# A two-layer decoder trunk: the mixer's token norm folded into the split operands

## The chip, the cores and the metric

The kernel runs on one NeuronCore of a Trainium2 chip. The metric is device microseconds of one execution, as the median of several runs. TensorE (PE in the profile) multiplies, with its own rows for weight loads (PEld); VectorE is DVE, ScalarE is ACT, GpSimd is POOL. SyncE (SP) issues nearly all DMA transfers, in the order in which they stand in its queue.

## The reference

Two layers work on x of 1024 tokens by 1024 features, in float32. What the change touches is the first part of a layer, the mixer:

```python
h = rmsnorm(x, norm_mix[l])                       # x * rsqrt(mean(x*x) + EPS) * g
proj = jnp.einsum('btd,de->bte', h, w_in[l])      # 1024 -> 4352
q, k, v, u, ug, ga, gb = jnp.split(proj, SPLITS, axis=-1)
q = partial_rope(rmsnorm(q, q_norm[l]), cos, sin) # per head of 64
k = partial_rope(rmsnorm(k, k_norm[l]), cos, sin)
a_out = sliding_window_attention(q, k, v, sinks[l])
c_out = conformer_conv(u, ug, ...)                # a = u * sigmoid(ug); depthwise conv of width 31; layernorm; silu; projection
merged = sigmoid(ga) * a_out + sigmoid(gb) * c_out
x = x + merged @ w_out[l]
```

A gated feed-forward with its own norm (`norm_ffn`, `w_gate_up`, `w_down`) follows and adds to x. Features lie on partitions in the kernel, tokens along the free axis, so x is eight tiles of 128 x 1024.

## The kernel before

**Precision.** Each float32 operand is split into a high part in fp32r (a rounded copy, made by ACT) and the remainder (a subtraction). `mm3` (L236) forms a product from three matmuls per step and half of the tokens: high by high, high by low, low by high. For weights, `fetch` (L120) loads a raw tile of 512 KB, ACT copies it to `wh` (L133) and POOL subtracts to `wl` (L134); there are two raw tiles, three of `wh` and two of `wl` (L1159).

**Stages of a layer.** The input projection has 34 column tiles, in the order of `INPROJ` (L1138); a tile is eight contraction steps of six matmuls, into a PSUM tile of 128 x 1024 out of a ring of two. The mixer's attention and its convolution run beside these tiles. Then come the two projections to x (`wcv`, `wout`), the feed-forward's up products and its down products, the last in seven block products p1 to p7 of which p3 is the last (L1124).

**The norm.** x is split after the product with the gain g, and without the token factor r = rsqrt(mean + eps): r is one number per token, and so can be put on a column of the result. In layer 0, `split_g` (L281) makes the two parts from each loaded tile of x, POOL squares the tile, DVE adds the squares to `acc` (L288). In layer 1 the same is done with half tiles as the down products release them (`done`, L1051): the tile goes to DRAM, ACT and DVE make the two parts, ACT squares, DVE adds. `norm_a` (L370) then takes token means by TensorE (`tokmean`, one column per 128 tokens), a power of -0.5 by POOL, a diagonal by DVE (`diag`, L308), and a product with a matrix of ones that spreads r over the partitions into the tile `R` of 128 x 1024. Values, conv values, conv gates and both sets of gates are multiplied by R as DVE takes them out of PSUM (L451, L473, L478, L724); ACT then makes the sigmoids in SBUF (L479, L725), and POOL multiplies conv value and gate (L482). Queries and keys aren't multiplied: their own norm per head cancels r, if its eps is scaled, which `e64` does (L373, L394).

**The first tiles.** Keys and values are computed together, step by step (L739 to L752). In layer 0 the steps follow the order of the loaded tiles; in layer 1 the first four steps are 4 to 7 in both halves, then the rest by halves, since p3 completes the tiles 0 to 3 of the second token half last.

**What sets the order.** TensorE's instructions are always in program order, as is DVE's from the first keys to the end of the attention (L754). The other engines' order comes from a planner that simulates the program with its own costs. Within the attention stage the program order is made from a clock written by hand: `tick()` (L227) advances it by one at each contraction step, and runs the events that are due; `after`, `at` and `when_free` set such events. The 32 attention units (four for each pair of heads) start 16 ticks after the first query tile, one every 6 ticks (L779). A unit computes scores into PSUM, DVE takes the maxima, ACT the exponentials, TensorE transposes, POOL masks the two parts by four selects (L684, L687), TensorE multiplies by the values. A query tile brings its own work: eviction and squares by ACT, four DMA moves for the rotation, two products and a power on POOL, sums and splits on DVE. The convolution is 31 taps for each of four tiles on DVE (L492, L496), one every 1.42 ticks, from 2 ticks after the first conv gate, when the tile `a` is handed over (6 ticks after the gate).

## Time and profile before

| | |
|---|---|
| median of three runs | 2698.68 us (2694.47 to 2700.15) |
| the profiled execution's own time | 2704.77 us |
| span in its profile | 2703.0 us |
| mean granted TensorE clock | 0.975 |
| busy: TensorE, DVE, ACT, POOL | 2588.6, 1843.6, 1190.6, 1601.5 us |
| first query tile leaves PSUM (layer 0, layer 1) | 96.11, 1437.67 us |

The rows of the profile give start, duration, engine, line, operation, output and inputs with their sizes; in square brackets stands the idle time before the instruction and what ended it. Rows of groups give count, busy time and mean duration, then that idle time. Matmuls are pipelined: two of them may overlap, so their pace is read from a run of many.

### The profile page before, as it was taken

How to read it: one execution, taken by the hardware profiler on the slowest of the kernel's cores; microseconds unless marked ns; L12 is line 12 of the kernel's file. 1: busy time of each engine (PE TensorE's matmuls, PEld its weight loads, DVE VectorE, ACT ScalarE, POOL GpSimd, SP SyncE). 2: the span in 40 equal slices, each digit the busy share in tenths (PEclk: the TensorE clock that was granted, in tenths of full speed). 3: DMA queues.
4: the chain of work that ended last, by engine and by line, in shares of the span. 5: the costliest groups of instructions: out<-in, count | busy, mean ns of one | idle time of the engine just before them, and what ended most of it. 6: DMA issues, size and time to landing. Idle time of an engine off the chain costs nothing.

```text
span 2703.0 us, 33316 instructions
## 1 busy us (share of the span) xinstructions
PE 2588.6 (96%) x11736; PEld 2118.2 (78%) x11736; DVE 1843.6 (68%) x2037; ACT 1190.6 (44%) x2299; POOL 1601.5 (59%) x1028
## 2 busy tenths in 40 slices
PE   7999999999999999999999999989999999999999
PEld 5777777788787888878777777778887788888887
DVE  6689998552567777845637899895616678778344
ACT  2266666742432323344523566668425222223443
POOL 7368776525256767765534777775252677767544
PEclk8999999999999999999999999989999999999999
DMA  3222222475244454476721222234752444455666
GB/s 129 57 66 58 82 80 67 158 271 208 90 164 147 168 179 156 160 269 218 238 67 52 65 88 65 74 93 156 252 203 94 179 168 146 162 179 193 223 223 210
DMA packets 137478, 395.83 MB, mean 146 GB/s; under 512 B 16160, under 2 KB 16416, under 8 KB 137312
## 3 DMA queue, kind: packets, MB, share of 16 engines
q1 hardware_dynamic: 137168, 393.63, 43.3%
q8 instruction: 92, 1.51, 0.2%
q14 instruction: 74, 0.61, 0.1%
q10 hardware_dynamic: 144, 0.09, 0.0%
HBM read 259.17 MB, written 115.34 MB: 139 GB/s over the span
## 4 chain that ended last, share of the span: by engine, by line
PE 64%; DVE 21%; DMA 4%; POOL 4%; issue 3%; ACT 2%; SPq 1%; DVEq 0%; ACTq 0%; POOLq 0%
PE b L850 40%; PE ps L242 20%; DVE y L496 9%; DVE mx L652 1%; DVE sc L648 1%; DVE q L610 1%; DVE acc L295 1%; DVE A L714 1%; DMA qs<-q 1%; PE po L702 1%; POOL q L385 1%; DVE pl L679 1%; DVE g L724 1%; DMA x<-xs 1%; POOL wl L134 1%
## 5 line engine op out<-in xcount | busy, mean ns | idle before, releaser
L151 POOL TENSOR_TENSOR plo<-fraw,phi 128x512 fp32r<-128x512 f32 x290 | 421.4, 1461 | 232.5 <-ACT phi L149 217.4
L134 POOL TENSOR_TENSOR wl<-raw,wh 128x1024 fp32r<-128x1024 f32 (+1 forms) x100 | 241.0, 2411 | 292.2 <-PE ps L242 250.3
L151 POOL TENSOR_TENSOR plo<-fs,phi 128x512 fp32r<-128x512 f32 x160 | 264.7, 1665 | 252.0 <-ACT phi L149 240.4
L496 DVE SCALAR_TENSOR_TENSOR y<-a,vec,y 128x1024 f32<-128x1024 f32 x240 | 402.6, 1678 | 3.6
L149 ACT CAST phi<-fraw 128x512 fp32r<-128x512 f32 x444 | 257.6, 618 | 246.7 <-POOL plo L151 133.6
L242 PE MATMUL ps<-hx,wh 128*128 128x512 f32 x1056 | 350.6, 414 | 7.2 <-ACT hx L283 7.2
L242 PE MATMUL ps<-lx,wh 128*128 128x512 f32 x1056 | 341.0, 405 | 0.8 <-DVE lx L284 0.8
L242 PE MATMUL ps<-hx,wl 128*128 128x512 f32 x1056 | 337.4, 401 | 4.5 <-POOL wl L134 4.5
L149 ACT CAST phi<-fs 128x512 fp32r<-128x512 f32 x160 | 95.4, 620 | 533.9 <-DVE fs L164 520.1
L151 DVE TENSOR_TENSOR plo<-fraw,phi 128x512 fp32r<-128x512 f32 x154 | 129.8, 848 | 191.5 <-ACT phi L149 189.3
L242 PEld LDWEIGHTS ps<-hx,wl 128*128 128x128 f32 x1056 | 206.7, 196 | 50.8 <-POOL wl L134 4.9
L850 PE MATMUL b<-plo,phi 128*128 128x512 f32 x616 | 241.1, 391 | 4.5 <-DVE plo L151 4.2
L242 PEld LDWEIGHTS ps<-lx,wh 128*128 128x128 f32 x1056 | 207.6, 197 | 48.3 <-DVE lx L284 1.5
L850 PE MATMUL b<-phi,plo 128*128 128x512 f32 x616 | 240.4, 390 | 0.0
L850 PE MATMUL b<-phi 128*128 128x512 f32 x616 | 240.4, 390 | 0.0
L242 PEld LDWEIGHTS ps<-hx,wh 128*128 128x128 f32 x1056 | 196.1, 198 | 43.1 <-ACT hx L283 7.2
L133 ACT CAST wh<-raw 128x1024 fp32r<-128x1024 f32 (+1 forms) x100 | 98.1, 981 | 175.7 <-PE ps L242 137.1
L656 ACT ACTIVATE sc<-sc,nm,fq 128x129 f32<-128x129 f32 x256 | 123.8, 486 | 70.4 <-DVE nm L654 69.9
L918 POOL TENSOR_TENSOR g<-g,u 128x512 f32<-128x512 f32 (+1 forms) x84 | 129.3, 1557 | 31.6 <-DVE u L971 25.2
L914 DVE TENSOR_TENSOR g<-g 128x512 f32<-128x512 f32 x88 | 103.9, 1181 | 62.8 <-POOL g L918 42.5
L850 PEld LDWEIGHTS b<-plo,phi 128*128 128x128 f32 x616 | 116.1, 188 | 31.8 <-DVE plo L151 7.8
L850 PEld LDWEIGHTS b<-phi 128*128 128x128 f32 x616 | 116.0, 188 | 24.3
(254 smaller groups left out, 6141.2 us busy)
## 6 DMA issues: line engine op xcount, KB each, us to landing
fraw<-wgu SPq DMA_DIRECT2D x88, 512.0 KB
raw<-win SPq DMA_DIRECT2D x68, 512.0 KB
act<-g SPq DMA_DIRECT2D x44, 512.0 KB
dw<-wdn SPq DMA_DIRECT2D x44, 512.0 KB
td<-g SPq DMA_DIRECT2D x44, 512.0 KB
sd<-dw SPq DMA_DIRECT2D x44, 512.0 KB
fraw<-sd SPq DMA_DIRECT2D x88, 256.0 KB
fraw<-td SPq DMA_DIRECT2D x88, 256.0 KB
```

What stands on the lines that cost most here:

```text
L133: nc.scalar.copy(wh, raw)
L134: nc.gpsimd.tensor_tensor(out=wl, in0=raw, in1=wh.bitcast(F32), op=ALU.subtract)
L149: nc.scalar.copy(hi, src)
L151: (eng or nc.gpsimd).tensor_tensor(out=lo, in0=src, in1=hi.bitcast(F32), op=ALU.subtract)
L242: nc.tensor.matmul(ps[:, sl], a[:, wc], b[:, sl], start=first and j == 0, stop=last and j == 2)
L295: (add or nc.gpsimd).tensor_tensor(out=acc, in0=acc, in1=sq, op=ALU.add)
L385: nc.gpsimd.tensor_tensor(out=src, in0=src, in1=ct, op=ALU.mult)
L496: nc.vector.scalar_tensor_tensor(out=y, in0=a[:, j:j + T], scalar=V(w0 + j), in1=y, op0=ALU.mult, op1=ALU.add)
L656: nc.scalar.activation(sc[:, n], sc[:, n], AF.Exp, bias=nm[:, n:n + 1], scale=fq[:, 4 * j + n:4 * j + n + 1], accum_out=den[:, n:n + 1])
L850: nc.tensor.matmul(ps, w[:, ai * P:(ai + 1) * P], x, start=first and j == 0, stop=last and j == 2, skip_group_check=True)
L914: nc.vector.tensor_tensor(out=o, in0=x, in1=y, op=ALU.subtract)
L918: nc.gpsimd.tensor_tensor(out=g[:, sl], in0=g[:, sl], in1=u[:, sl], op=ALU.mult)
```

## The change

The token factor goes into x before the split. `token_scale` makes the diagonal for 512 tokens, a matmul with ones spreads it in a PSUM bank, and `normed` multiplies a half tile in place by g and by that bank, copies the high part and subtracts the low one. `R` and `e64` go; so do the products with R, and ACT takes gates, conv gates and values straight from PSUM. The conv tile `a` is now a product by DVE of the PSUM tile of `u` with the gate, and each gate is computed ahead of its value tile.

The first three tiles are conv gate 0, conv value 0 and keys, computed together for the first token half and then for the second, both in the step order 4 to 7, 0 to 3 (`KLATE`). In layer 0 the loads of x are in half tiles, all first halves ahead of the first weights, and ACT makes the squares. In layer 1 the first half is scaled during p3, from reloads of the tiles that `done` has written to DRAM; the second half within the three tiles' steps, again from reloads. Values follow as a tile of their own. `wl` gets a third buffer.

```diff
+    def token_scale(pss, acc, n):
+        for b in range(4):
+            o = n * HALF + b * P
+            nc.tensor.matmul(pss[:, b:b + 1], acc[:, o:o + P], onesD, start=True, stop=True)
+        tmp = sm.tile([P, 4], F32, tag="rse4", name="rse")
+        nc.vector.tensor_scalar(out=tmp, in0=pss[:, 0:4], scalar1=1.0, scalar2=EPS, op0=ALU.mult, op1=ALU.add)
+        rtok = sm.tile([P, 4], F32, tag="rtok4", name="rtok")
+        nc.gpsimd.tensor_tensor(out=rtok, in0=tmp, in1=mhalf[:, 0:4], op=ALU.pow)
+        dg = t4("dg")
+        nc.vector.tensor_tensor(out=dg[:, 0:HALF].rearrange("p (b c) -> p b c", b=4),
+                                in0=ident.unsqueeze(1).broadcast_to([P, 4, P]),
+                                in1=rtok.unsqueeze(2).broadcast_to([P, 4, P]), op=ALU.mult)
+        return dg
+
+    def normed(x, g, pb, out):
+        nc.vector.scalar_tensor_tensor(out=x, in0=x, scalar=g, in1=pb, op0=ALU.mult, op1=ALU.mult)
+        h, l_ = out
+        nc.scalar.copy(h, x)
+        nc.vector.tensor_tensor(out=l_, in0=x, in1=h.bitcast(F32), op=ALU.subtract)
...
-                fetch(1)
-                for e in range(KD):
-                    nc.sync.dma_start(xin[e], xT[e])
-                    if e == 0:
+                for n in range(2):
+                    for e in KLATE:
+                        nc.sync.dma_start(xin[e][:, hv[n]], xT[e][:, hv[n]])
+                    if n == 0:
                         fetch(2)
...
+            square(0)
+            dg = token_scale(ps_o("pss"), acc, 0)
+            pb = ps_pT("pb")
+            nc.tensor.matmul(pb, onesmat, dg[:, 0:HALF], start=True, stop=True)
+            for e in KLATE:
+                normed(xin[e][:, 0:HALF], V(V_GM + e), pb, [t[:, 0:HALF] for t in xs[e]])
+            square(1)
+        ws = [next_w() for _ in range(3)]
+        ps3 = [pstile(), pstile(),
+               psm.tile([P, 4, 2 * P], F32, tag="S", bufs=1, name="psk").rearrange("p a b -> p (a b)")]
+        for k in KLATE:
+            for w, ps in zip(ws, ps3):
+                mm3(ps, w, kcols(k), xs[k], k == KLATE[0], k == KLATE[-1], (0,))
+            if k == KLATE[1]:
+                dg = token_scale(ps_o("pss"), acc, 1)
+            if k == KLATE[4]:
+                pb = ps_o("pb")
+                nc.tensor.matmul(pb, onesmat, dg[:, 0:HALF], start=True, stop=True)
+                for e in KLATE:
+                    if l == 0:
+                        x = xin[e][:, HALF:]
+                    else:
+                        x = t4("xr")[:, 0:HALF]
+                        nc.sync.dma_start(x, xnx[e][:, HALF:])
+                    normed(x, V(V_GM + e), pb, [t[:, HALF:] for t in xs[e]])
+        for k in KLATE:
+            for w, ps in zip(ws, ps3):
+                mm3(ps, w, kcols(k), xs[k], k == KLATE[0], k == KLATE[-1], (1,))
...
-            nc.vector.tensor_tensor(out=ssb, in0=pss[:, 0:16].rearrange("p (b h) -> p b h", h=2),
-                                    in1=e64.unsqueeze(2).broadcast_to([P, NB, 2]), op=ALU.add)
+            nc.vector.tensor_scalar(out=ssb.rearrange("p b h -> p (b h)"), in0=pss[:, 0:16], scalar1=1.0,
+                                    scalar2=HD * EPS, op0=ALU.mult, op1=ALU.add)
...
-            after(1 if l else NA + 0.5, lambda: rope(k32))
+            rope(k32)
...
-            after(9, lambda: rope_add(k32))
-            when_free('pT', 11, lambda: turn(0))
-            when_free('pT', 13, lambda: turn(1))
+            after(10, lambda: rope_add(k32))
+            when_free('pT', 13, lambda: turn(0))
+            when_free('pT', 15, lambda: turn(1))
...
-            nc.vector.tensor_tensor(out=v32, in0=ps, in1=R, op=ALU.mult)
+            nc.scalar.copy(v32, ps)
...
         def conv_g(c, ps):
             ug = t4("ug")
-            nc.vector.tensor_tensor(out=ug, in0=ps, in1=R, op=ALU.mult)
-            nc.scalar.activation(ug, ug, AF.Sigmoid)
+            nc.scalar.activation(ug, ps, AF.Sigmoid)
+            held_g[c] = ug
+
+        def conv_u(c, ps):
             a = ap_.tile([P, T + CW - 1], F32, tag="a", bufs=2, name="a")
             nc.gpsimd.memset(a[:, 0:CW - 1], 0.0)
-            nc.gpsimd.tensor_tensor(out=a[:, CW - 1:], in0=held_u.pop(c), in1=ug, op=ALU.mult)
-            after(6, lambda: avals.update({c: a}))
+            nc.vector.tensor_tensor(out=a[:, CW - 1:], in0=ps, in1=held_g.pop(c), op=ALU.mult)
+            avals[c] = a
...
         def gate(ps):
             g = t4("g")
-            nc.vector.tensor_tensor(out=g, in0=ps, in1=R, op=ALU.mult)
-            nc.scalar.activation(g, g, AF.Sigmoid)
+            nc.scalar.activation(g, ps, AF.Sigmoid)
...
+        conv_g(0, ps3[0])
+        after(1.5, lambda: (conv_u(0, ps3[1]), tap(clock[0])))
+        keys(ps3[2])
         tick()
...
-            g = vec[l + 1][:, V_GM + e:V_GM + e + 1]
-            h, l_ = (t[:, hv[n]] for t in xs[e])
-            nc.scalar.activation(h, x, AF.Copy, scale=g)
-            nc.vector.scalar_tensor_tensor(out=l_, in0=x, scalar=g, in1=h.bitcast(F32),
-                                           op0=ALU.mult, op1=ALU.subtract)
...
+                if name == "p3" and not last and p in (2, 4):
+                    if p == 2:
+                        dg = token_scale(bk[4], acc, 0)
+                    else:
+                        nc.tensor.matmul(bk[5], onesmat, dg[:, 0:HALF], start=True, stop=True)
+                        for k in range(KD):
+                            x = da.tile([P, HALF], F32, tag="x", bufs=8, name="x")
+                            nc.sync.dma_start(x, xnx[k][:, h0])
+                            normed(x, vec[l + 1][:, V_GM + k:V_GM + k + 1], bk[5], [t[:, h0] for t in xs[k]])
...
-INPROJ = [W_K, W_V, _u[0], _ug[0], 0, _u[1], _ug[1], 1, _gb[0], _u[2], 2, _ug[2], _ga[0], 3, _gb[1], _ga[1],
-          4, _u[3], _ga[2], 5, _ug[3], _ga[3], 6, _gb[2], _ga[4], 7, _gb[3], _ga[5], _gb[4], _gb[5],
+INPROJ = [_ug[0], _u[0], W_K, W_V, 0, _ug[1], _u[1], 1, _gb[0], 2, _ug[2], _u[2], _ga[0], 3, _gb[1], _ga[1],
+          4, _ug[3], _ga[2], 5, _u[3], _ga[3], 6, _gb[2], _ga[4], 7, _gb[3], _ga[5], _gb[4], _gb[5],
           _ga[6], _ga[7], _gb[6], _gb[7]]
+KLATE = [4, 5, 6, 7, 0, 1, 2, 3]
...
-WRAW, WHI, WLO, T4 = 2, 3, 2, 4
+WRAW, WHI, WLO, T4 = 2, 3, 3, 4
```

More of the change, by code (lines that the diff above doesn't have):

```diff
@@ new lines, in square @@
+            def square(n):
+                a = acc[:, hv[n]]
+                for e in KLATE:
+                    x = xin[e][:, hv[n]]
+                    sq = a if e == KLATE[0] else t4("sq")[:, 0:HALF]
+                    nc.scalar.activation(sq, x, AF.Square)
+                    if e != KLATE[0]:
+                        nc.vector.tensor_tensor(out=a, in0=a, in1=sq, op=ALU.add)
+            square(0)
+            dg = token_scale(ps_o("pss"), acc, 0)
+            pb = ps_pT("pb")
+            nc.tensor.matmul(pb, onesmat, dg[:, 0:HALF], start=True, stop=True)
@@ L357, in trunk @@
         nc.sync.dma_start(st_, sinT)
-        e64 = mp.tile([P, NB], F32, name="e64")
-        R = mp.tile([P, T], F32, name="R")
         lsum = mp.tile([P, T], F32, name="lsum")
@@ L368, in trunk @@
         nc.gpsimd.memset(rot, 0.0)
-        def norm_a():
-            rtok = sm.tile([P, NB], F32, tag="rtok", name="rtok")
-            msx = rsqrt_eps(tokmean(ps_o("pss"), acc, onesD), rtok)
-            nc.vector.tensor_scalar(out=e64, in0=msx, scalar1=HD * EPS, scalar2=None, op0=ALU.mult)
-            dg = diag(rtok)
-            [when_free('pT', 3 + 2 * n, lambda n=n: bcast_half(ps_pT("pb"), dg, R, n)) for n in range(2)]
         def inproj():
@@ L736, in mul_a @@
             nc.sync.dma_start(mA[i], g)
-        wk, wv = next_w(), next_w()
-        psk = pstile()
-        psv = psm.tile([P, 4, 2 * P], F32, tag="S", bufs=1, name="psv").rearrange("p a b -> p (a b)")
-        both = ((wk, psk), (wv, psv))
-        steps = [(k, (0, 1), both) for k in range(KD)]
-        if l > 0:
-            steps = [(k, (0, 1), both) for k in range(4, KD)] + [(k, (0,), both) for k in range(4)]
-            steps += [(k, (1,), (x,)) for x in both for k in range(4)]
-        for i, (k, ns, wps) in enumerate(steps):
-            for w, ps in wps:
-                mm3(ps, w, slice(k * P, (k + 1) * P), xs[k], i == 0, k == steps[-1][0], ns)
-            if i < 7:
-                tick()
-        after(0 if l else NA, norm_a)
         dve = ExitStack()
         dve.enter_context(tc.manual_schedule(engines={mybir.EngineType.DVE}))
-        keys(psk)
+        conv_g(0, ps3[0])
+        after(1.5, lambda: (conv_u(0, ps3[1]), tap(clock[0])))
+        keys(ps3[2])
         tick()
@@ L761, in project @@
                 queries(j, ps)
+            elif j == W_V:
+                values(ps)
             elif W_U <= j < W_UG:
-                conv_u(j - W_U, ps)
+                after(0.5, lambda: conv_u(j - W_U, ps))
             elif W_UG <= j < W_GA:
@@ L770, in project @@
                 nc.sync.dma_start(sB[j - W_GB], gate(ps))
-        for idx, j in enumerate(INPROJ[2:-TAIL]):
-            if idx == 0:
-                after(NV_, lambda: values(psv))
+        for j in INPROJ[3:-TAIL]:
             project(j)
-            if idx == 1:
-                tap(clock[0] + 2)
-            if idx == 2:
+            if j == W_Q:
                 start = clock[0] + S0
```

18 lines of the change are left out of this document (7 added, 11 removed).

## The prediction

> **What bounds the kernel now.** I read the page first: span, engines, chain.
>
> ```profile
> span 2703.0 us, 33316 instructions
> PE 2588.6 (96%) x11736; PEld 2118.2 (78%) x11736; DVE 1843.6 (68%) x2037; ACT 1190.6 (44%) x2299; POOL 1601.5 (59%) x1028
> PE 64%; DVE 21%; DMA 4%; POOL 4%; issue 3%; ACT 2%; SPq 1%; DVEq 0%; ACTq 0%; POOLq 0%
> ```
>
> TensorE bounds it, with VectorE (DVE) second. Next came the windows over the attention stage of each layer, TensorE's waits in it, and windows around single waits.
>
> ```profile
> 90.00:550.00 460.00, 426.74 (x2101) 353.57 (x2100) 388.02 (x433) 283.34 (x655) 304.76 (x197) 0.94 0.28 86
> 1430.00:1890.00 460.00, 425.28 (x2102) 352.67 (x2101) 386.72 (x432) 281.91 (x653) 306.15 (x196) 0.95 0.28 86
> ```
>
> Busy times stand in the order PE, PEld, DVE, ACT, POOL, then the granted clock. In 460 us TensorE is idle 33 us, and a mean clock of 0.94 loses 0.06 x 460 = 28 us more: 61 us per layer. Its waits in the first of these windows (us, times, longest):
>
> ```profile
> PE po L702 <- POOL ph L687: 9.2, 4, 3.0
> PE S L636 <- DMA qs<-q: 6.3, 6, 2.2
> PE po L702 <- DVE ssb L394: 5.7, 3, 2.2
> PE S L636 <- DVE sc L648: 4.5, 4, 2.7
> PE po L702 <- POOL pl L687: 4.3, 4, 1.2
> ```
>
> Each wait also costs clock, as two short windows show:
>
> ```profile
> 117.00:127.00 10.00, 8.21 (x33) 6.41 (x32) 8.55 (x6) 2.74 (x5) 3.38 (x2) 0.83 0.33 92
> 220.00:232.00 12.00, 9.30 (x38) 7.64 (x37) 11.78 (x17) 9.04 (x21) 6.64 (x6) 0.72 0.13 38
> ```
>
> In the first, 10 - 8.21 = 1.8 us of idle (the waits for the first query's `qs`) brought a clock of 0.83, 1.7 us lost; in the second 2.7 us brought 0.72, 3.4 lost. I price every wait over 1 us at itself plus 1.7. DVE is busy 84% of the stage; the waits on `qs`, `ssb` and `sc` (16.5 us) end on late DVE work, those on `ph` and `pl` (13.5 us) on POOL's order.
>
> **The change: DVE work in the attention stage.** The products with R leave DVE: 14 gates and 3 conv gates per layer in this stretch. The product for `u` stays on DVE and takes POOL's multiply with it.
>
> ```profile
> L724 DVE TENSOR_TENSOR g<-ps,R 128x1024 f32<-128x1024 f32 x14 | 17.1, 1224 | 14.4 <-PE ps L242 14.1
> L478 DVE TENSOR_TENSOR ug<-ps,R 128x1024 f32<-128x1024 f32 x3 | 3.7, 1224 | 1.4 <-PE ps L242 1.3
> L496 DVE SCALAR_TENSOR_TENSOR y<-a,vec,y 128x1024 f32<-128x1024 f32 x120 | 200.5, 1671 | 1.8
> L724 DVE TENSOR_TENSOR g<-ps,R x32: 1223/1224/1225, 156.7 to 1912.5; 128x1024 f32<-128x1024 f32 x32
> ...
> L646 DVE TENSOR_TENSOR sc<-S,mneg x8: 411/414/420, 130.4 to 491.2; 128x256 f32<-128x256 f32 x8
> 389.53 0.41 DVE L646 TENSOR_TENSOR sc<-S,mneg 128x256 f32<-128x256 f32 x1
> ```
>
> DVE loses 17.1 + 3.7 = 20.8 us of work and 15.8 us in which it stood for a tile's end. The written clock also starts the conv taps earlier. Before, the first tap stands near tick 30 and the first query tile ends at 32, 1.4 taps in (1.42 ticks each). After, taps start at 1.5 and that tile ends at 17: 11 taps in. So 9.5 taps x 1.67 = 16 us move into the opening, where DVE has room. None of this counts one for one, since DVE binds only where TensorE waits for it. How far it does, I read from the pace of the heads: L646 with the 128x256 mask runs once per head. The first five periods take (389.5 - 130.4) / 5 = 51.8 us, the last two (491.2 - 389.5) / 2 = 50.8. In the last two DVE has slack, and the waits are POOL's. I take 50.8 as the floor that POOL's unchanged query work sets: 5 x 1.0 = 5 us, plus the first query's wait of 1.8, and 1.7 of clock, which is for late DVE too: 8.5 us per layer, 17 in both. Bounds: nothing, if POOL's waits fill in; 16.5 + 28 x 16.5 / 33 = 30 us per layer, if every wait on late DVE goes with its clock.
>
> [...]
>
> The gates' sigmoids remain and their operand moves to PSUM; a query's eviction by ACT from PSUM (L583) takes 1.1 us against 1.06 for a sigmoid, so ACT's work is unchanged. What is new is that a sigmoid waiting for its tile has exponentials queued behind it. I take no cost, because ACT's evictions of query tiles showed no wait at all (0.0 before L583); upper bound below, among the rivals. The scalar eps in place of `e64`, values' copy on ACT (2 per run) and the third `wl` buffer I take at nothing: they lie behind TensorE's stream. Lower bound of the buffer: it lets POOL run a tile ahead, a gain put into the second rival.
>
> **The opening of layer 0** (to the first query tile in PSUM).
>
> ```profile
> 4.65 1.04 ACT L133 CAST wh<-raw 128x1024 fp32r<-128x1024 f32 x1 [2.13 <-DMA raw<-win]
> 17.02 1.15 ACT L283 ACTIVATE hx<-xi,vec 128x1024 fp32r<-128x1024 f32 x1 [0.20 <-DMA xi<-xT]
> 96.11 1.11 ACT L583 ACTIVATE q<-ps,vec 128x1024 f32<-128x1024 f32 x1
> ```
>
> The operations that the new chain repeats, from the groups:
>
> ```profile
> L134 POOL TENSOR_TENSOR wl<-raw,wh 128x1024 fp32r<-128x1024 f32 x84 | 220.2, 2623 | 210.8 <-PE ps L242 194.8 <-issue 11.2 <-ACT wh L133 4.1
> L1066 DVE TENSOR_TENSOR acc<-acc,x 128x512 f32<-128x512 f32 x14 | 15.1, 1078 | 4.3 <-ACT x L1065 3.9
> L299 PE MATMUL pss<-onesD,acc 128*128 128x1 f32 x16 | 3.6, 353 | 3.1 <-DVE acc L295 3.1
> L305 POOL TENSOR_TENSOR rtok<-rse,mhalf 128x8 f32<-128x8 f32 x1 | 1.7, 1657 | 5.0 <-DVE rse L304 5.0
> L310 DVE TENSOR_TENSOR dg<-ident,rtok 128x1024 f32<-128x1024 f32 x1 | 3.4, 3401 | 1.6 <-POOL rtok L305 1.6
> L317 PE MATMUL pb<-dg,onesmat 128*128 128x512 f32 x24 | 12.4, 599 | 1.7 <-DVE dg L310 1.7
> L1059 DVE SCALAR_TENSOR_TENSOR lx<-x,vec,hx 128x512 fp32r<-128x512 f32 x16 | 14.7, 939 | 0.9 <-ACT hx L1058 0.8
> 547.89 150.94 PE ps L242 x660
> ```
>
> Ten transfers of 512 KB landed between 4.65 and 17.0, 1.37 us each. Eight half tiles are four of these: 8.8. Then, with ACT's 512 columns at half of L283's 1.15, square 0.6, add 1.1, half of the token means 1.8, power 1.7, half of the diagonal 1.7, broadcast 0.6, scaled product 0.9, copy 0.6: first matmul at 17.8, while today it runs from the first tile on. It isn't that which sets the pace, but the third weight tile. With two raw buffers its transfer waits for the first `wl`, and it lands as the eleventh, at 18.4; plus 1.05 and 2.6 its `wl` is there at 22.1, where TensorE stands at the ninth matmul. From there 232 matmuls at 150.94 / 660 = 0.229 us: 53.1. Other matmuls and clock in such an opening I take from layer 1 (below): 12.2. At the values tile all three `wh` buffers are held to the last of the interleaved steps: 1.05 + 2.6, less six matmuls and four that don't need `wl` (2.3), leaves 1.4, and 1.7 of clock. Half of the transposes' waits remain, 1.6. Sum 92.1 against 96.1: -4 us. Bounds -9 (third tile early) and +4 (the sigmoid and a table load ahead of the `wh` copy, 2.3, and second-half squares on DVE).
>
> **The opening of layer 1.**
>
> ```profile
> 1333.00 2.47 DVE L1069 TENSOR_TENSOR x<-x,b 128x512 f32<-128x512 f32 x4
> 1346.80 1.78 DVE L1066 TENSOR_TENSOR acc<-acc,x 128x512 f32<-128x512 f32 x1
> 1365.50 0.63 PE L242 MATMUL ps<-hx,wh 128*128 128x512 f32 x2
> 1371.75 0.69 DVE L1066 TENSOR_TENSOR acc<-acc,x 128x512 f32<-128x512 f32 x1 [2.89 <-ACT x L1065]
> 1437.67 1.11 ACT L583 ACTIVATE q<-ps,vec 128x1024 f32<-128x1024 f32 x1
> ```
>
> ```profile
> PE pb L317 <- DVE dg L310: 1.7, 1, 1.7
> PE ptv L457 <- DVE kd L428: 1.5, 1, 1.5
> PE ptk L424 <- DVE k L400: 1.2, 1, 1.2
> PE pk L438 <- DVE kl L441: 0.6, 1, 0.6
> ```
>
> Today 72.2 us, of which 240 x 0.229 = 55.0 are dense and 5.0 waits: the 12.2 used above. The wait for `dg` goes, with its clock: -3.4. The second half's token mean comes after 18 matmuls, at 1369.6, but `acc` is complete at 1372.4, since each square waits for its tile's way out to DRAM: +2.8, and 1.7 of clock. The weights' hand-over costs +3.1 as above; the key rope starts earlier: -1.6. In the last down product the first half's mean stands after 36 matmuls, at 1335.5 + 8.2 = 1343.7; `acc` is done at 1348.6, less four low-half products (3.8) that go: +1. DVE does 16 operations there for the normed halves instead of 8, about 15 us at L1059's 939 ns, hidden under 30 us of products as long as the reloads keep up; uncovered they would cost the rest of the bound. SP carries 16 more reloads of 256 KB. Sum +4, bounds -3 and +12.
>
> [...]
>
> **Sum.** -4 + 4 - 17 = -17 us, against the profiled execution's 2704.8: 2687.8. It stands 6.1 above the median of the runs shown, so on that scale 2681.6; I say 2681.
>
> **The rivals.** (1) POOL's waits fill what DVE gives up. For: the last two periods, with slack on DVE, are hardly shorter. Against: the first query's wait is not POOL's. Only the openings remain, 0: 2698, chance 0.15. (2) POOL's waits go as well, since `wl` no longer waits for the tile before and one multiply per conv tile has left POOL. For: `wl` is POOL's largest piece and often waits for TensorE; against, the query's own chain fills POOL without it. Half of 13.5 us and of its clock (28 x 13.5 / 33 = 11.5) is 12.5 per layer, 25 in both: 2656, chance 0.22. (3) Slower: ACT takes DVE's place in standing for tiles. The 15.8 us per layer now spent by DVE in front of L724 and L478 become waits of ACT's queue, with exponentials behind, then the transposes of TensorE. With clock for six long ones (10) that is 26 per layer; it decides from a third of it reaching TensorE, which eats the 8.5. With two thirds, +17 - 8.5 per layer: 2715, chance 0.15. [...] (4) The third buffer and early taps do nothing and the openings reach their bounds, +16: 2714 less what DVE gives, about 2700, chance 0.06.
>
> **How the numbers follow.** The forecast has 0.42, as 2666 to 2693. What a measurement here can tell from no change is 0.2%, 5.4 us: 2693.3 to 2704. Faster: 0.42, 0.22 and a little of (1): 0.68. Same: most of (1) and (4), 0.15. Slower: (3) and the rest, 0.17. The range reaches from beyond rival 2 (2640) into rival 3 (2709), leaving out about 0.1 on either side.
>
> **What would show it.** Right: the head period in the first five heads falls to about 50.8 while the waits on `ph` and `pl` stay; the first matmul is near 18 us and a wait for `wl` ends near 22; first query tile near 92; layer 1's opening 3 us longer, with a wait on `acc`. Wrong: waits on `sc` by ACT (L672) that grow past 5 us; POOL waits that vanish; layer 1's opening longer by over 12 us.

## The result, and the profile after

The changed kernel takes 2719.14 us (2716.01 to 2721.36, four runs) against 2699.41 us in runs beside it: a ratio of 1.0076, with a 95% interval of 1.0058 to 1.0093. It is 20 us slower, and the forecast of 2681 us was wrong in sign. Its profiled execution took 2718.8 us. The page begins so (span; busy times):

```profile
span 2717.0 us, 33332 instructions
PE 2586.0 (95%) x11736; PEld 2115.8 (78%) x11736; DVE 1796.0 (66%) x2044; ACT 1191.7 (44%) x2321; POOL 1552.5 (57%) x1014
```

VectorE gave up 47.6 us of work and GpSimd 49.0, TensorE's work is the same, and yet the span grew by 14.0 us. The window over layer 0's attention stage, to be set beside that of before (the same time on the clock, though the stage starts 7.7 us later):

```profile
90.00:550.00 460.00, 424.41 (x2111) 351.68 (x2112) 360.95 (x423) 282.00 (x658) 293.62 (x192) 0.94 0.27 82
```

VectorE is busy for 361 us there instead of 388, at the same granted clock of 0.94. It doesn't run freer for that: its waits for ACT's copy of the transposed scores grew from the first line (before) to the second (after), while its 14.1 us of waits for the ends of gate tiles are gone.

```profile
DVE pl L679 <- ACT ph L674: 6.6, 3, 3.2
DVE pl L728 <- ACT ph L723: 36.4, 12, 7.1
```

TensorE's waits over the whole kernel (us in all, times, longest), first two of before, then those of after:

```profile
PE po L702 <- POOL ph L687: 18.4, 8, 3.0
PE pT L672 <- ACT sc L663: 5.1, 9, 1.1
...
PE pT L721 <- ACT sc L712: 15.3, 10, 2.6
PE ptk L476 <- DVE vv L514: 12.8, 3, 7.0
PE pss L319 <- DVE acc L378: 12.4, 1, 12.4
PE po L751 <- POOL pl L736: 11.8, 9, 2.5
PE po L751 <- DVE ssb L446: 11.4, 6, 3.7
...
PE b L883 <- DVE plo L151: 6.8, 3, 3.1
PE pssl L299 <- DVE A L763: 5.5, 2, 2.8
...
PE po L751 <- POOL ph L736: 0.9, 2, 0.6
```

To place the time I cut each trace at five instructions that both kernels have: the eviction of the first query tile in each layer, the first matmul of the convolution's projection (`wcv`) in each layer, and the last down product of layer 0. The lengths in us, from the first rows of those instructions:

| stretch | before | before, second profile | after |
|---|---|---|---|
| start to first query, layer 0 | 96.1 | 96.7 | 103.8 |
| to the convolution's projection, layer 0 | 474.8 | 471.4 | 470.2 |
| to the last down product, layer 0 | 794.4 | 791.6 | 805.3 |
| to first query, layer 1 | 72.4 | 71.1 | 77.7 |
| to the convolution's projection, layer 1 | 474.7 | 471.9 | 470.2 |
| to the end | 790.7 | 789.5 | 789.8 |

The second profile of before is a run of its own (below). The change loses 7 us in the first opening, 16 to 20 between layer 0's convolution projection and the first query of layer 1, and gains only 3 to 9 in the two attention stages together.

**Layer 0's opening** in the timeline after (start, duration, engine):

```profile
12.45 1.84 PE L319 MATMUL pss<-onesD,acc 128*128 128x1 f32 x8 [12.45 <-DVE acc L378]
13.05 2.36 POOL L134 TENSOR_TENSOR wl<-raw,wh 128x1024 fp32r<-128x1024 f32 x1 [10.20 <-ACT wh L133]
...
15.36 1.04 POOL L323 TENSOR_TENSOR rtok<-rse,mhalf 128x4 f32<-128x4 f32 x1
16.43 2.83 DVE L325 TENSOR_TENSOR dg<-ident,rtok 128x512 f32<-128x512 f32 x1 [1.95 <-POOL rtok L323]
19.32 2.08 PE L382 MATMUL pb<-dg,onesmat 128*128 128x512 f32 x2 [5.03 <-DVE dg L325]
21.43 5.36 DVE L332 SCALAR_TENSOR_TENSOR xi<-xi,vec,pb 128x512 f32<-128x512 f32 x8
23.14 0.79 PE L242 MATMUL ps<-hx,wh 128*128 128x512 f32 x1 [1.75 <-ACT hx L334]
24.11 2.37 POOL L134 TENSOR_TENSOR wl<-raw,wh 128x1024 fp32r<-128x1024 f32 x1 [5.40 <-ACT wh L133]
27.31 3.69 DVE L335 TENSOR_TENSOR lx<-xi,hx 128x512 fp32r<-128x512 f32 x6
28.05 0.79 PE L242 MATMUL ps<-lx,wh 128*128 128x512 f32 x1 [4.12 <-DVE lx L335]
```

The first matmul stands at 23.1 us and the second at 28.1, since VectorE makes all eight scaled products before the first remainder. The power waits for GpSimd to finish a weight remainder that the planner put ahead of it.

**The keys.** The same timeline later in that opening:

```profile
77.58 0.17 DVE L446 TENSOR_SCALAR ssb<-pssh 128x16 f32<-128x16 f32 x1 [1.90 <-PE pssh L443]
80.21 2.89 POOL L448 TENSOR_TENSOR fk<-ssb,mhalf 128x16 f32<-128x16 f32 x1
83.07 2.38 POOL L134 TENSOR_TENSOR wl<-raw,wh 128x1024 fp32r<-128x1024 f32 x1
83.13 2.36 DVE L470 TENSOR_SCALAR f<-fk 128x16 f32<-128x16 f32 x1 [5.38 <-POOL fk L448]
93.00 1.09 PE L476 MATMUL ptk<-ident,k 128*128 128x128 f32 x4 [5.33 <-DVE vv L514]
```

VectorE, in program order, stands 5.4 us for the key factor, with convolution taps and the values' remainders (`vv`) queued behind; TensorE then waits 5.3 us for the bank that `vv` empties. In layer 1 the two waits are 7.1 and 7.0 us.

**The last down product** and layer 1's first token mean, in TensorE's timeline:

```profile
1350.02 1.05 PE L319 MATMUL b<-onesD,acc 128*128 128x1 f32 x8 [2.67 <-DVE acc L1094]
1371.30 0.54 PE L883 MATMUL b<-plo,phi 128*128 128x512 f32 x1 [2.21 <-DVE plo L151]
1386.62 1.05 PE L319 MATMUL pss<-onesD,acc 128*128 128x1 f32 x8 [2.76 <-DVE acc L1094]
```

Three waits of over 2 us stand where before had one of 0.8 for a weight piece and the 1.7 for `dg` that the prediction quotes.

### The profile page after: what moved, and what is told of

Its sections match the earlier page's. It is cut to its first block, busy times and chain, and to the rows that moved or that the text cites. A ratio compares the mean times of both kernels' runs of the same rounds, so it can differ in the third digit from the quotient of the medians.

```text
span 2717.0 us, 33332 instructions
## 1 busy us (share of the span) xinstructions
PE 2586.0 (95%) x11736; PEld 2115.8 (78%) x11736; DVE 1796.0 (66%) x2044; ACT 1191.7 (44%) x2321; POOL 1552.5 (57%) x1014
## 4 chain that ended last, share of the span: by engine, by line
PE 35%; DVE 8%; ACT 3%; issue 2%; POOL 1%; DMA 1%; SPq 0%; DVEq 0%; ACTq 0%; POOLq 0%
PE b L883 23%; PE ps L242 10%; DVE y L545 4%; ACT sc L705 1%; DVE mx L701 1%; DVE sc L697 0%; PE po L751 0%; DVE pl L728 0%; PE psk L242 0%; DVE A L763 0%; PE pssh L443 0%; DMA xn<-x 0%; POOL rot L438 0%; POOL wl L134 0%; DVE q L659 0%
## 5 line engine op out<-in xcount | busy, mean ns | idle before, releaser
L947 DVE TENSOR_TENSOR g<-g 128x512 f32<-128x512 f32 x88 | 107.1, 1217 | 63.4 <-POOL g L951 46.1
L951 POOL TENSOR_TENSOR g<-g,u 128x512 f32<-128x512 f32 (+1 forms) x84 | 128.6, 1550 | 31.0 <-DVE u L1004 24.6
```

The costliest lines, as they stand in the source:

```text
L947: nc.vector.tensor_tensor(out=o, in0=x, in1=y, op=ALU.subtract)
L951: nc.gpsimd.tensor_tensor(out=g[:, sl], in0=g[:, sl], in1=u[:, sl], op=ALU.mult)
```

## The experiments

**Four single edits.** The first puts the key factor's product off, so that VectorE doesn't stand for it; the second puts the token mean and its spreading in p3 two steps later; the third moves the convolution's whole norm, which had the wait on `A`; the fourth is the kernel before with only the gates changed (it leaves out the factor R in the gates).

```diff
# a_f8 (changed kernel)
-                nc.vector.tensor_scalar(out=f8, in0=fk, scalar1=8.0, ...)
+                after(4, lambda: nc.vector.tensor_scalar(out=f8, in0=fk, scalar1=8.0, ...))
# a_p3 (changed kernel)
-                if name == "p3" and not last and p in (2, 4):
+                if name == "p3" and not last and p in (4, 6):
# a_ln (changed kernel)
-LN1 = 7
+LN1 = 10
# b_gates (kernel before)
-            nc.vector.tensor_tensor(out=g, in0=ps, in1=R, op=ALU.mult)
-            nc.scalar.activation(g, g, AF.Sigmoid)
+            nc.scalar.activation(g, ps, AF.Sigmoid)
```

> The changed kernel with one edit: the product of the key norm's factor with 8 (L470) is put on VectorE four ticks after the power that it reads, not right behind the token sums. Theory: VectorE stands 5.4 and 7.1 us at this product, waiting for POOL's power, with conv taps and the values' remainders queued behind, and TensorE's waits at the key transposes (5.3 and 7.0 us, and 3.4 us of clock each) follow from it. Then these waits fall below 1.5 us each, the openings of the layers become 8 to 10 us shorter each, and the time is 18 us (15 to 21) below the changed kernel. Rival: the key's rotation on POOL, or the taps themselves, hold the transposes; then the wait stays, or goes to another tile, and the time is within 5 us of the changed kernel.

> The changed kernel with the first half's token mean and its spreading, which stand in the last down product after 3 and 5 of its steps, moved to after 5 and 7. Theory: TensorE's wait for acc there (2.7 us, and 1.7 of clock) comes from the place alone, since each square waits for its tile's way to DRAM; it goes, and the time is 4 us (3 to 6) below the changed kernel, with the wait for a weight remainder (2.6 us) still there. Rival: that block is held by the reloads and by VectorE's 16 added operations; then later scaling runs into the first tiles of layer 1, what the acc wait gives is lost there, and the time is within 2 us or longer.

> The changed kernel with the conv's layer norm begun 10 ticks after the last tap, not 7. Theory: with the taps done earlier, the layer norm's token sums meet an attention unit that still holds the same PSUM bank; TensorE waits 2.8 us there in each layer and loses 3.4 us to the clock and 0.7 in the sums. Half a unit's period later it doesn't meet it: the stretch from the eighth head to the first matmul of the conv projection falls from 87.4 to about 80 us in each layer, the time by 14 us (8 to 15). Rival: ScalarE is late there because it takes the gates from PSUM, whatever the tick; then another wait takes the place and the time is within 3 us.

> The kernel before, with one part of the change alone: both sets of gates and the conv gates leave PSUM by ScalarE's sigmoid. It leaves out the factor R in these gates. Theory of the prediction: relief of VectorE (20.8 us of products and 15.8 us of standing per layer) shortens the attention stage by 5 to 10 us per layer, read as the seven head periods that sum to 360.8 us before, and the time is 2680 to 2690 against 2699. Rival: the gain of the changed kernel (10 us per layer in these periods) comes from taps that start earlier and the new tile order; then the periods stay at 358 to 363 and the time within 4 us of before. Second rival: ScalarE stands for the tiles instead, and waits at the transposes grow by more than is gained: longer than before.

Measured: `a_f8` 2711.94 us, ratio 1.0045 (1.0027 to 1.0062), so 7.2 us off the changed kernel; `a_p3` 2713.85, 1.0052 (1.0036 to 1.0068), 5.3 off; `a_ln` 2720.66, 1.0074 (1.0057 to 1.0092), nothing; `b_gates` 2700.16, 1.0002 (0.9992 to 1.0012) of before, nothing.

The waits behind the key factor fell from 12.8 to 5.6 us in `a_f8`:

```profile
PE ptk L476 <- DVE vv L514: 5.6, 4, 2.3
```

So the mechanism stands, at less than half of the 18 us expected: the openings give 5.2 and 3.8 us where 8 to 10 each were expected, since a wait of 2.3 us stays in each. `a_p3` came as expected in time, but not by the wait on `acc` alone: the wait for a weight piece, which was to stay, went too (2.2 to 0.3 us). `a_ln` took the wait on `A` down to 1.3 us in all, but others came in its place: the stretch from the eighth head to the convolution's projection stays at 88.6 us, and its expectation fell.

`b_gates` lies between its theory and its rival. The seven head periods, read as in the prediction, fall from 360.8 to 355.0 us, but the time stays, where 2680 to 2690 was expected. The attention stages take 471.0 and 471.3 us, as in the second profile of before, because the stretch behind the eighth head grows from 84.2 to 87.6 us. VectorE's waits for ACT's copy are there with the gates alone (31.5 us in the same window).

**Edits added up, and the opening in written-out order.** `c_fp` joins the first two edits. `c_alt` adds VectorE's order (product of tile e+1 before the remainder of tile e), `c_open` GpSimd's order too. `b_again` is the kernel before, unchanged.

```diff
# c_alt: in place of the loop over normed(...)
+            with tc.manual_schedule(engines={mybir.EngineType.DVE}):
+                late = None
+                for e in KLATE:
+                    nc.vector.scalar_tensor_tensor(out=x, in0=x, scalar=V(V_GM + e), in1=pb, ...)
+                    nc.scalar.copy(h, x)
+                    if late:
+                        nc.vector.tensor_tensor(out=late[1], in0=late[0], in1=late[2].bitcast(F32), op=ALU.subtract)
+                    late = (x, l_, h)
...
# c_open: and the power ahead of the weight remainders
+            with tc.manual_schedule(engines={mybir.EngineType.Pool}):
+                dg = token_scale(ps_o("pss"), acc, 0)
+                fetch(2)
```

> The kernel before, unchanged, for a second profiled execution. Its first profile lies 5.3 us above the median of its own runs (2704.8 against 2699.4), while the profiles of the changed kernels lie within 3.5 us of theirs. If the 5 us are in one stage, that stage was overstated when the change was costed. Theory: they lie in cold windows of TensorE in the attention stage or in the opening, so this profile has a span near 2698 (2695 to 2701), with from the first query's eviction to the first matmul of the convolution's projection 472 to 475 us in each layer, and 793 to 796 us from there to the last down-projection matmul of layer 0. Rival: every stage is as before to within 1 us and the span is near 2703 again.

> The changed kernel with two edits that were each tried alone: the key factor's product put off by four steps (alone -7.2 us) and the token mean and its spreading in the last down product two steps later (alone -5.3 us). Theory: the two waits stand at different places and nothing else depends on both, so the gains add: -12.5 us, 2706.6 us (2703 to 2710), ratio to the kernel before 1.0027. Rival: both shorten the way into layer 1's opening, and part of the second gain came back there as a wait of its own (+1.4 us when the mean was put off alone); then the gain is 8 to 9 us, 2710 to 2711.

> The former, and in layer 0's opening VectorE's order written out: scaled product of tile e+1, then the remainder of tile e, instead of all eight products and then the remainders. Theory: the first remainder comes at about 23.5 us in place of 27.3, the second matmul near 24.2 in place of 28.1, and then the third weight tile's low part (26.5 us) is the next wait, of 1 to 2 us; the first query is evicted 2 to 3 us earlier than without the edit (96 against 98.9 in the kernel with the key factor put off). Rival: TensorE only trades one wait for several short ones with a cold clock, and the first query is where it was within 1 us.

> The former, and GpSimd's order written out as well in layer 0's opening: the power of the first half's mean ahead of the two weight remainders, not behind the first. Theory: the power starts when its operand is there (near 14.5 us, 0.9 us earlier), the diagonal with it, and the first matmul at about 22; the third raw weight tile still waits for a weight remainder, so its low part ends near 25 to 26. The first query is evicted 3 to 5 us earlier than with the two late edits alone, so 2701 to 2704 us, ratio 1.001 to 1.002. Rival: the opening is bound by the three weight tiles (loading and splitting), not by the mean's chain, and moves under 1.5 us.

Measured: `b_again` 2693.96 us in its one run; `c_fp` 2707.30, ratio 1.0030 (1.0021 to 1.0039), `c_alt` 2705.49 in one run, `c_open` 2705.34, 1.0022 (1.0013 to 1.0031). The two edits add, 11.8 us of 12.5. VectorE's order alone (`c_alt`) moved the first query from 98.9 to 96.6 us, as expected. With GpSimd's order too (`c_open`) it stands at 97.7, 1.2 us before `c_fp`, where 3 to 5 were expected. The power starts earlier there, at 13.9 us, but VectorE then spends 4.4 us on three additions of the second half's squares ahead of the first scaled product, and the first matmul comes at 23.6. The third weight tile's low part ends at 28.8, and TensorE waits 0.7 us for it. So the rival's number is met, and its cause in part. In the total, 2 us between `c_fp` and `c_open` aren't clear of noise.

`b_again` has a span of 2692.2 us and a granted clock of 0.983, the first profile of before 2703.0 and 0.975. Both parts of its expectation fell: the span is shorter than the 2695 us put as its lower end, and the 10.8 us aren't in one stage but in all stretches except the first, 3 of them in each attention stage. My forecast was made against an execution 5.4 us above the median of its kernel, and this one lies 4.9 below it, so each stage is known to within some 3 us and no better.

**The waits left.** `d_best` is `c_open` with three more edits (the expectation says four and names these three): the factor of 8 goes into the power's operand, so that VectorE's small product is gone; the squares in the last down product go to a tile of their own, so that they don't wait for the store of the tile that they overwrote; and a one-column sigmoid loads ACT's table before the first gate tile is done (after the change a load of 1.28 us stood right ahead of that tile's sigmoid).

```diff
+        def headnorm(sq, f, c=1.0):
...
-                nc.vector.tensor_scalar(out=f8, in0=fk, scalar1=8.0, ...)
+                headnorm(sq, f8, 1.0 / HD)
...
-                nc.scalar.activation(x, x, AF.Square)
+                s = t4("sq")[:, 0:HALF]
+                nc.scalar.activation(s, x, AF.Square)
...
+        nc.scalar.activation(warm, xs[KLATE[-1]][0][:, T - 1:T].bitcast(F32), AF.Sigmoid)
```

> The changed kernel with the mean in the last down product two steps later and the opening of layer 0 in written-out order (as in the last run), and four more edits at the waits that were left: the key factor comes out of the power itself (its operand is scaled by 1/64 where the epsilon is added, and the product by 8 is gone), the squares in the last down product go to a tile of their own and no longer wait for the store of the tile they overwrote, and the sigmoid's table is loaded before the first gate tile is done (a one-column sigmoid of the last normed tile). Theory: the transposes' wait behind the key factor (2.4 us a layer, with a cold clock), the wait for acc in layer 1's opening (2.7) and the wait for the first gate (1.9 a layer) go, each with up to 1.7 us of clock: -4 to -5 in layer 0's opening and -8 in layer 1's and the last down product, so 2693 to 2697 us, at or a little below the kernel before (2699). Rival: waits of the next operand stand right behind each (the second half's scaled tiles, the transposes' own hand-overs), as in the written-out opening, which gave 1.2 us where 4 were expected; then 2701 to 2704.

Measured: 2697.12 us, ratio 0.9995 (0.9986 to 1.0004). That is the top of the expected range: with these edits the changed design stands level with the kernel before, 22 us below the change as it was made. The first query is at 95.7 us, and the stretch from layer 0's convolution projection to layer 1's first query is 868.9 us, against 883.0 after the change and 862.7 and 866.8 before it. The wait on `acc` in layer 1's opening is gone, and the transposes' first wait in layer 0 is 1.4 us in place of 5.3:

```profile
85.47 0.63 PE L494 MATMUL ptk<-ident,k 128*128 128x128 f32 x4 [1.37 <-DVE vv L532]
```

**What sets the pace of the heads.** Now the attention stage, by leaving work out of one engine at a time: ACT's four scaled copies of each unit, half of VectorE's taps (in the changed kernel and in the one before), and one of GpSimd's four masks.

```diff
# e_act
-                for n in range(4):
-                    nc.scalar.activation(sc[:, n, 0:P], sc[:, n, 0:P], AF.Copy, scale=ri[:, n:n + 1])
# e_dve, b_dve
+                    if j % 2 == 0:
                         nc.vector.scalar_tensor_tensor(out=y, in0=a[:, j:j + T], scalar=V(w0 + j), ...)
# e_pool
+                if k == 0:
                     mo = ap_.tile([P, 4, P], F32R, tag=f"mo{k}", ...)
                     nc.gpsimd.affine_select(out=mo, ...)
                 own.append(mo)
```

> The changed kernel without the softmax's division (the four scaled copies of every unit on ScalarE are left out, 393 ns each, 6.3 us a head; the output lacks the division). Question: what holds the seven head periods at 356 us (366 before the change). Theory: with VectorE relieved, ScalarE's chain from the scores to the transposes is the wait that comes last (7.9 us of TensorE's waits in these seven heads are for the scaled copies); without them the seven periods fall by 8 to 14 us, to 342 to 348. Rival: VectorE's taps and score chain still set the pace; then the waits for the scaled copies move to the next consumer and the periods stay within 4 us of 356.

> The changed kernel with every second convolution tap left out on VectorE (15 of 31 per channel tile, 1.66 us each, some 80 us of 163 in these seven heads; the convolution is incomplete). Theory: VectorE was the bound before and no longer is after its relief, so taking another 11 us a head from it gives little: the seven periods fall from 356 by 3 to 8 us, from the waits that the factor operand and the additions of the unit outputs still cause (11 us). Rival: VectorE still sets the pace, and the periods fall by 20 us or more. In the stretch from the eighth head to the convolution's projection the wait for the mean's operands (2.8 us and its clock) goes in either case.

> The changed kernel without one of the four masks of every unit on GpSimd (the own block's mask of the remainder; the high part's masked tile is used in its place, so the remainder of the own block is left out of the output; 0.89 us each, 3.6 us a head). Theory: the waits for the masked remainder (6.1 us in the seven heads) fall to 2 or less, and the periods by 4 to 7 us, to 349 to 352. Rival: those waits stand in the shadow of the additions and the copies that end at the same time, and the periods stay within 2 us of 356.

> The kernel before with every second convolution tap left out on VectorE (the convolution is incomplete), as in the run on the changed kernel, where the seven head periods fell from 356 to 331.5 us. Question: whether the change's relief of VectorE is what shortened the heads from 366 to 356. Theory: it is, and with VectorE far from full the rest of the change is worth little there, so this kernel's seven periods come to 331 to 336 us, within 5 us of the changed kernel's. Rival: the tile order or the gates' path shortens the heads by itself; then the difference of 10 us stays, 340 or more.

Each fence is one window of one kernel, from the first score matmul of the first head to that of the eighth in layer 0: length, then busy PE, PEld, DVE, ACT, POOL, clock. Before, second profile:

```profile
119.10:484.20 365.10, 327.87 (x1649) 272.71 (x1649) 333.57 (x368) 227.10 (x547) 258.82 (x163) 0.96 0.25 76
```

After:

```profile
129.50:485.40 355.90, 327.98 (x1651) 272.60 (x1651) 303.04 (x349) 226.20 (x550) 247.15 (x160) 0.95 0.26 78
```

`e_act`, without the scaled copies:

```profile
128.50:488.00 359.50, 325.42 (x1652) 273.47 (x1652) 301.99 (x349) 193.22 (x438) 251.64 (x160) 0.95 0.26 78
```

`e_dve`, half of the taps:

```profile
123.40:454.70 331.30, 319.27 (x1652) 269.72 (x1652) 229.78 (x298) 224.95 (x550) 225.79 (x160) 0.97 0.28 84
```

`e_pool`, three masks of four:

```profile
128.80:476.50 347.70, 326.80 (x1652) 273.26 (x1652) 296.88 (x349) 226.73 (x550) 214.93 (x133) 0.96 0.26 79
```

`b_dve`, before with half of the taps:

```profile
118.30:446.70 328.40, 315.38 (x1648) 268.32 (x1648) 241.80 (x311) 226.02 (x548) 229.52 (x163) 0.97 0.28 84
```

Taking 33.0 us of work from ACT made the heads 3.6 us longer, so the waits of TensorE that end on ACT's copies aren't a bound of their own; my theory fell, and the waits moved on to GpSimd's masks (6.1 us in the same window after the change, here 14.1):

```profile
PE po L749 <- POOL pl L734: 14.1, 8, 4.3
```

Taking 73.3 us from VectorE gave 24.6 us, a third (GpSimd's busy time fell by 21.4 with it); taking 32.2 from GpSimd gave 8.2, a quarter (VectorE's own busy time fell by 6.2 with it) and a little more than the 4 to 7 expected. Here my theory for `e_dve` fell too: VectorE still sets the pace after the change. What it expected behind the eighth head fell as well: the wait on `A` stays, 2.8 us, and that stretch takes 88.9 us. The change itself took 30.5 us from VectorE (and 11.7 from GpSimd) and gave 9.2, at about the same rate. And with VectorE relieved, the kernel before has heads of 328.4 us, 2.9 shorter than the changed one and a little below the 331 to 336 expected: where VectorE has room, the rest of the change is worth nothing. That is the theory of `b_dve`. Where VectorE is full, two parts can be told apart: the gates alone (`b_gates`) take 20.1 us from VectorE and give 3.8, and what comes on top with the earlier taps and the new order is 10.4 us less on VectorE and 5.4 shorter heads. That no part of these 5.4 us is due to the order itself isn't shown. Total times of these four, in one run each: 2724.56, 2660.65, 2700.25 and 2624.21 us.

**Where the heads' gain goes.** Between the first and the eighth head the change gains 9 to 12 us a layer. It gives 3 back between the first query and the first scores (25.3 us against 22.1 and 22.7), where back-transposes of the keys now stand (TensorE waits 1.8 us for one of them), and 4.7 between the eighth head and the convolution's projection (88.9 against 84.2). There the trace after shows TensorE waiting for a PSUM bank:

```profile
511.38 0.28 PE L751 MATMUL po<-pl,vv 128*128 128x256 f32 x1
...
516.16 0.86 DVE L763 TENSOR_TENSOR A<-po,sh 64x256 f32<-64x256 f32 x2
517.16 2.52 PE L299 MATMUL pssl<-onesC,s 128*128 128x1 f32 x16 [2.75 <-DVE A L763]
```

The sums for the variance need the bank that a unit's output holds until VectorE has added it up, which starts 4.8 us after the last matmul. Three runs on `d_best` moved these sums or the key's back-transposes:

```diff
-            when_free('po', 4 + LC[3] + 6, var)
+            when_free('po', 4 + LC[3] + 8, var)        # f_var and f_all; 10 in g_var
...
-                when_free('po', 4, lambda: back(g, kdv, 1))
+                when_free('po', 5, lambda: back(g, kdv, 1))   # f_all only
```

> The former best variant with one more edit: the column sums for the convolution norm's variance two steps later, so that their bank of PSUM is no longer still held by a unit's output (TensorE waits 2.7 us there for the additions, once a layer, after the eighth head). Theory: the part of the heads' gain that is lost after the eighth head hangs on this one wait; the stretch from the eighth head to the convolution's projection falls from 87.4 and 90.3 us to 84 to 85, as before the change, so 5 to 8 us in all: 2689 to 2693 us, ratio 0.997 to 0.998. Rival: as when the whole norm was put off by three steps, a wait of the units comes in its place (the copies for the transposes, the masks), the stretch stays at 87 to 89 and the time within 2 us of 2697.

> The former, and the second of each pair of key back-transposes one step later, so that it no longer waits for VectorE's remainder of the first (1.8 us once a layer between the first query and the first scores). Theory: the stretch from the first query to the first scores falls from 25.4 to 23 us in each layer (the transposes' own work stays), another 3 to 5 us: 2685 to 2690. Rival: the keys then come later to the first scores, or the next dense tile is ended by another wait; the stretch stays within 1 us and the time within 2 us of the former.

> The best variant with the variance's column sums four steps later. The edit by two steps left the order of TensorE's instructions as it was (the sums still stood three tiles behind the same unit's output matmuls, because the bank counts as taken until then), so it told nothing; by four steps they stand right behind the next unit's score matmuls, some 7 us after the additions they waited for. Theory: the wait of 2.7 us and its clock go in both layers, the stretch from the eighth head to the convolution's projection falls from 87.4 and 90.3 us to 84 to 85, and the time to 2689 to 2693 us. Rival: a wait of a unit takes its place; the stretch stays at 87 to 89 and the time within 2 us of 2697 to 2698.

Measured: `f_var` 2698.51 us, 0.9994 (0.9984 to 1.0004); `f_all` 2701.97, 1.0013 (1.0003 to 1.0022); `g_var` 2690.01, 0.9970 (0.9960 to 0.9980). `f_var` left TensorE's order as it was, so it tests nothing and is a second measurement of `d_best`. In `f_all`, where 2685 to 2690 us were expected, the back-transposes waited longer (6.6 us in all instead of 3.6), and the stretch before the first scores grew to 28.2 us. In `g_var` the sums stand behind the next scores, and there is no wait before them:

```profile
507.82 0.86 DVE L781 TENSOR_TENSOR A<-po,sh 64x256 f32<-64x256 f32 x2
509.55 1.84 PE L307 MATMUL pssl<-onesC,s 128*128 128x1 f32 x16
```

The stretch is 84.5 us in both layers, as before the change, the attention stages take 466.7 and 465.8, and stretch and time came as expected. So what was lost after the eighth head hung on this one wait. `g_var` is the fastest of the complete kernels here, 7 us or 0.3% below the kernel before. Its last stretch, from layer 1's convolution projection on, takes 795.0 us against 789.5 and 790.7 before; that I can't explain.

## Why the prediction was wrong

Against the first profile of before, the three terms of the sum measured +7.7, +16.2 and -9.1 us where -4, +4 and -17 were forecast; the last stretch adds -0.9.

**Layer 0's opening (forecast -4, measured +7.7).** The chain to the first matmul was put at 17.8 us and took 23.1. `acc` was complete at 12.4 instead of 10.5; the power started 0.9 us late behind a weight remainder on GpSimd; the diagonal took 2.83 us instead of 1.7, beside GpSimd's next remainder (the second half's took 0.69); the spreading took 2.08 instead of 0.6, which was the mean of one record where a spreading has two. The third weight tile's low part, put at 22.1, ended at 26.5. The largest single piece was not in the sum at all: the key factor, for which VectorE stands with taps and values' remainders behind. I had counted half of the transposes' waits, 1.6 us, and moved 16 us of taps into the opening "where DVE has room", without asking what the taps and `vv` would queue behind. Putting off that product alone took the first query from 103.8 to 98.6 us in `a_f8` and to 98.9 in `c_fp`: 5 of the 11.7 us by which the forecast of 92.1 was missed. By the prediction's own sum, the low part's 4.4 us are most of the rest.

**Layer 1's opening with p3 (forecast +4, measured +16 to +20).** The wait on `acc` was named and came as put (2.8 us). Two things failed. "The key rope starts earlier: -1.6" was taken as a gain, where the key factor's wait grew to 7.0 us. And the normed halves in p3, "hidden under 30 us of products", weren't: from p3's first product to its last it is 39.9 us against 30.4 and 30.3 in the two profiles of before, with a wait for `acc` of 2.7 and one for a weight piece of 2.2, each followed by 1.7 us lost to the clock (0.76 over 7 us, 0.79 over 8). The stretch that ends with p3 is 11 to 14 us longer; the other 2 to 3 us are in the first block, p1, and no run looked into them. `a_p3` got 8.4 of that stretch back by standing two steps later, and lost 1.3 again in the opening behind.

**The attention stage (forecast -17, measured -3 to -9).** The reading of the first heads was right: measured as in the prediction, on the masks, their five periods fell from 51.8 to 50.8 us. But 50.8 isn't a floor: the five lie between 46.1 and 54.7 us, and the last two, which were to stay, fell from 50.8 to 48.5. The cause was mainly VectorE's relief, as put. What failed is the step from the period to the stage: I took the two ends of the stage as unchanged. They lost some 7.5 us a layer, 4.7 of it on one bank of PSUM; without that wait, in `g_var`, the two stages gain 11 to 17 us together, where 17 was forecast. That POOL's query work sets a floor isn't borne out either: with half of the taps on VectorE the heads take 47.3 us each.

**The signs of the rivals.** TensorE's waits on ACT grew past the 5 us that I had set as a sign of rival 3, from 5.1 to 15.3, and those on `ph`, the sign of rival 2, fell from 18.4 to 0.9 while those on `pl` grew from 8.9 to 11.8. Neither rival is the cause of the loss. Rival 3 has ACT standing for tiles, and it doesn't: the 13 gate sigmoids of the first window after the change have 0.1 us of idle before them in all, and their table loads 0.2.

```profile
L773 ACT ACTIVATE g<-ps 128x1024 f32<-128x1024 f32 x13 | 13.3, 1026 | 0.1
```

Nor did shorter ACT work help, in `e_act`, and the heads, which rival 3 has longer, became shorter. Who stands is VectorE, for ACT's copies (36.4 us, above). What that costs, and whether the sigmoids ahead in ACT's queue make it so, isn't shown.

**The price of a wait** held in size, but not case by case. Two windows of after, before and behind the wait at 517:

```profile
505.00:517.00 12.00, 9.41 (x49) 7.47 (x47) 5.24 (x10) 10.61 (x27) 6.05 (x7) 1.00 0.38 128
517.00:529.00 12.00, 11.84 (x53) 10.18 (x53) 3.18 (x7) 5.75 (x9) 5.08 (x4) 0.72 0.20 68
```

2.75 us of idle are followed by a clock of 0.72 over 12 us, 3.4 us lost. In `g_var` both such windows have 1.00, and without the wait the stretch is 2.9 and 5.8 us shorter than in `d_best`; I had priced such a wait at 4.4. But the price isn't the same for every wait: the 2.2 us in p3 lost 1.7, and the one left at the key transposes in `a_f8` (its row, then a window from before its start) lost nothing.

```profile
89.30 0.63 PE L476 MATMUL ptk<-ident,k 128*128 128x128 f32 x4 [2.34 <-DVE vv L514]
87.00:98.60 11.60, 8.44 (x45) 6.40 (x46) 9.83 (x14) 2.66 (x5) 0.00 (x0) 1.00 0.13 45
```

So the length of a wait alone doesn't tell its price: 2.2 and 2.75 us were followed by a lower clock, and 2.34 wasn't.

**The scale.** I took 6.1 us off because the profile of before lay above its median. The profile of after lies 0.4 us below its own, so the traces show +14.0 where the medians show +19.7.

## What to carry to other kernels

When a moved step gets a new producer, list what stands behind it on the consumer's engine, at the place where it moves to: here waits of 2 to 7 us in program order turned a gain into a loss, and mending them, with the smaller edits beside them, brought back 29 us. A period that shortens in the middle of a stage is a gain of the stage only if its two ends are costed as well. Where several engines are nearly full, find out by leaving work out what a microsecond of each is worth: here about a third for VectorE, a quarter for GpSimd, nothing for ACT, though ACT's copies ended the longest of TensorE's waits in all. Such a number is rough, since work left out on one engine changed another's busy time here as well (GpSimd's by 21.4 us, VectorE's by 6.2).

## What the runs showed of the hardware

A product of 128 x 16 numbers on VectorE took 2.36 us (`f<-fk` above) where the one on the same shape from PSUM took 0.17 (`ssb<-pssh`). It began 0.06 us after a GpSimd remainder had begun and ended with it, 85.49 against 85.45, and the same in layer 1 (2.37 us). In `c_open`, where the product stands later, it takes 2.36 us again, 0.06 behind the start of a remainder. In the kernel before, where GpSimd started nothing within 2.1 us after the power, the same product (L418) took 0.17 us in both layers. So here the small product cost as much as the GpSimd operation of 128 x 1024 that started just before it (2.38 us); why isn't shown.

Two executions of the same kernel lay 10.8 us apart in span with granted clocks of 0.975 and 0.983, spread over all stages; differences between single profiles below that tell nothing of a total, while the length of the seven head periods repeated within 1.3 us in the eleven profiles that keep the changed kernel's heads (355.6 to 356.9 in layer 0).
